# A second chunk by seven products in mixer B's output projection, and more weight sums by transfers

## The chip, the core and the metric

One core of a Trainium2 chip runs the whole kernel. The metric is the time of one launch on the device in microseconds; the median of three runs counts. The core's engines work from their own instruction streams and wait for one another by semaphores: TensorE (PE in the profile; PEld is its load of the stationary operand) multiplies matrices into PSUM, VectorE (DVE) and ScalarE (ACT) do elementwise work, GpSimd (POOL) a little of it, and SyncE (SP) issues nearly all loads of weights. GpSimd's queue also issues transfers, among them those that add to their destination.

## The reference

It is an encoder of two layers over 256 positions of width 2048, in float32. Each layer adds a token mixer and a gated MLP to the residual stream, each behind an RMS norm:

```python
h = x
for i in range(DEPTH):
    hn = rms_norm(h, mix_norm[i])
    ...
    h = h + (mixer_a or mixer_b)(hn, ...)   # A in layer 0, B in layer 1
    h = h + conv_ffn(rms_norm(h, ffn_norm[i]), w_up[i], conv_w[i], conv_b[i], w_down[i])
return rms_norm(h, final_norm)
```

Mixer B computes `qkv = h @ w_qkv` (2048 by 9216), dilated sliding-window attention in three groups of eight heads with a relative bias, weighs the groups, and projects `y @ w_o` (3072 by 2048). The MLP is `u = h @ w_up` (2048 by 11264), a depthwise convolution of width three over positions, `silu(gate) * val`, and `@ w_down` (5632 by 2048).

## The kernel before

**Precision.** A float32 product is made of three TensorE products. A weight block `raw` (128 partitions by 1024) is split into a high part `wh`, a rounded copy by ScalarE (line 128), and a low part `wl = raw - wh` by VectorE (line 129), and the activations are split the same way; PE then multiplies high by high, low by high and high by low. Every weight of the model goes through this once, and it is most of what ScalarE and VectorE do. `raw` blocks live in six buffers that are reused in the order in which they came free. Split pieces live in a ring of NHL = 3 pairs, and four in the down-projections, which add one.

**Seven products.** A projection works on column blocks of 512 outputs and on "chunks" of 512 inputs. The two halves of the positions (128 rows each) and a pair of column blocks form a 2 by 2 block product, and for some chunks it is done by seven products with sums of the blocks instead of eight (`project_pair`, line 215). A unit of work is either a column unit `("c", chunk, i)`, four 128x512 positions of the plain product (12 matmuls), or a product unit `("P", chunk, p)` with p from 1 to 7 (6 matmuls). The list `units` is the order of PE's work. The weight operands of products 1, 2, 3 are the chunk's blocks 11, 21, 22; those of 5, 7, 6, 4 are sums that are made in place: 11 += 12, 12 += 22, 22 += 11, 21 += 22 (`sums_behind`, lines 255 to 268). Each sum is an addition of 128x1024 by VectorE (line 253), or a transfer on GpSimd's queue that adds to its destination (`onto`, line 249): from DRAM into 12 (the sum for product 7), or from block 22 into 21 in SBUF (for product 4). The argument `by_dma` names the products whose sums go by transfer; without it VectorE makes all four, one unit ahead (`prepare`, line 270).

**Who uses it.** In each FFN the down-projection runs in two halves, six and five chunks long, and each half over two pairs of column blocks. The first pair of a half starts while the last activations are still being made ("late"). Chunks 0, 2 and 4 of the first half and 0 and 2 of the second go by seven products. The function `weave` spreads the column units of the other chunks among the products: evenly in the first half, after every product in the second. The first halves make one sum per chunk by transfer (7), the second halves two (7 and 4). Ahead of a second half's up-projection stands a block of seven of its own (`seven`, line 405, with the units of lines 735 to 739). Mixer B's output projection (`out_proj`, line 870) has six chunks and two pairs; chunk 2 goes by products, with all four sums on VectorE. Its activation sums are made by `make_forms` (line 427) behind the last heads.

**What sets the order.** The units and the order of the code fix PE's and GpSimd's streams. Small jobs (residual sums, convolution, forms) are generators that `step()` advances between units. A scheduler then orders each engine's instructions, and the splits and sums of weights are put 45 places ahead (`high_priority`). SP issues the loads in order: a load whose buffer isn't free yet holds up those behind it. At the end of a pair `combine` (line 555) adds the product accumulators to the residual stream; accumulators not made of products are added at line 576. `place_blocks` (line 386) copies transposed blocks; a string of four letters says which engine takes each copy ("p" GpSimd, "a" ScalarE, "v" VectorE).

## Time and profile before

| | |
|---|---|
| median of 3 runs | 2234.03 us (2233.73 to 2235.28) |
| the profiled execution | 2236.12 us, span 2234.3 us, granted clock 0.998 |
| first FFN, first half's down-projection, pair 1 and pair 2 | about 527 to 589 and 589 to 652 us |
| first FFN, block of seven ahead of the second half | about 652 to 696 us |
| mixer B's output projection, pair 1 and pair 2 | about 1387 to 1454 and 1454 to 1518 us |
| second FFN, first half's down-projection, pair 1 and pair 2 | about 1780 to 1842 and 1842 to 1904 us |

A row of a timeline begins with its start and duration in microseconds; a bracket at its end is the time that the engine idled before it, and what ended the wait. A group's row ends with busy time, mean nanoseconds of one, and idle time before it. A row of the windows has each engine's busy time in the stretch with its instructions in brackets, then the granted clock, the share of the transfer engines and GB/s.

### The profile page before, as it was taken

To read this page: it belongs to the slowest core of one execution; us is meant where nothing else is said; L and a number is where in the kernel's file an instruction comes from. 1 tells how busy PE (TensorE), PEld (TensorE's weight loads), DVE (VectorE), ACT (ScalarE), POOL (GpSimd) and SP (SyncE) were. 2 spreads that over 40 slices of the span, in tenths; PEclk is the share of its full clock that TensorE was granted. 3 is DMA by queue.
4 is the path that set the end of the run, shared out by engine and by line. 5 is a ranking of instruction groups with operands and counts; after the bars stand their busy time and mean duration, and the time that the engine had idled before them with its cause. 6 is when DMAs were issued, how large, how long until landed. Compare 5 with 4: busy or idle time off the path is not lost. (4 is left out here: it accounts for less than half of the span.)

```text
span 2234.3 us, 29271 instructions
## 1 busy us (share of the span) xinstructions
PE 2218.5 (99%) x9997; PEld 1835.6 (82%) x9997; DVE 1848.7 (83%) x2543; ACT 1563.9 (70%) x2411; POOL 349.9 (16%) x507
## 2 busy tenths in 40 slices
PE   9999999999999999999999999999999999999998
PEld 7888888888778888888888888888888888888886
DVE  6777778889998888879877988796888899988897
ACT  6665677777557777767876877576777765677764
POOL 2211112211001111111340213010101100001111
PEclk9999999999999999999999999999999999999999
DMA  8444656766766556766655565555665677665675
GB/s 301 160 151 148 202 189 211 233 209 190 234 213 209 194 195 192 244 204 204 217 179 191 170 207 173 189 194 187 195 195 192 205 224 221 208 195 191 222 235 163
DMA packets 129670, 448.99 MB, mean 201 GB/s; under 512 B 17664, under 2 KB 18432, under 8 KB 129520
## 3 DMA queue, kind: packets, MB, share of 16 engines
q1 hardware_dynamic: 119744, 425.64, 57.9%
q0 software_dynamic: 9344, 20.92, 4.9%
q8 instruction: 78, 1.28, 0.2%
q14 instruction: 72, 0.59, 0.1%
q10 hardware_dynamic: 432, 0.56, 0.1%
HBM read 438.11 MB, written 6.29 MB: 199 GB/s over the span
## 5 line engine op out<-in xcount | busy, mean ns | idle before, releaser
L129 DVE TENSOR_TENSOR wl<-raw,wh 128x1024 fp32r<-128x1024 f32 x873 | 1068.6, 1233 | 265.5 <-ACT wh L128 261.5
L128 ACT ACTIVATE wh<-raw 128x1024 fp32r<-128x1024 f32 x873 | 915.6, 1057 | 457.3 <-PE acc L155 162.9
L154 PE MATMUL acc<-wl,xh 128*128 128x512 f32 x1664 | 649.3, 390 | 2.4 <-DVE wl L165 2.1
L153 PE MATMUL acc<-wh,xh 128*128 128x512 f32 x1664 | 649.0, 391 | 0.0
L155 PE MATMUL acc<-wh,xh 128*128 128x512 f32 x1664 | 648.8, 390 | 0.0
L154 PEld LDWEIGHTS acc<-wl,xh 128*128 128x128 f32 x1664 | 313.0, 188 | 68.6 <-DVE wl L165 2.6
L155 PEld LDWEIGHTS acc<-wh,xh 128*128 128x128 f32 x1664 | 312.7, 188 | 64.4
L153 PEld LDWEIGHTS acc<-wh,xh 128*128 128x128 f32 x1664 | 312.8, 188 | 64.0
L318 PE MATMUL acc<-wh,ah 128*128 128x512 f32 x730 | 284.7, 390 | 0.6 <-DVE h L576 0.6
L320 PE MATMUL acc<-wh,al 128*128 128x512 f32 x730 | 284.3, 389 | 0.0
L393 POOL COPY u<-t 32x256 f32<-32x256 f32 x176 | 110.5, 628 | 804.2 <-DVE t L628 796.1
L323 PE MATMUL acc<-wl,ah 128*128 128x512 f32 x730 | 205.2, 390 | 0.5 <-DVE wl L129 0.5
L318 PE MATMUL acc<-wh,xh 128*128 128x512 f32 x416 | 162.8, 391 | 0.0
L320 PE MATMUL acc<-wh,xh 128*128 128x512 f32 x416 | 162.0, 389 | 0.0
L318 PEld LDWEIGHTS acc<-wh,ah 128*128 128x128 f32 x730 | 137.0, 188 | 30.1 <-DVE h L576 1.4
L323 PEld LDWEIGHTS acc<-wl,ah 128*128 128x128 f32 x730 | 136.7, 188 | 30.2 <-DVE wl L129 2.0
L395 ACT ACTIVATE u<-t 32x256 f32<-32x256 f32 x352 | 147.7, 420 | 18.3 <-DVE t L628 10.5
L320 PEld LDWEIGHTS acc<-wh,al 128*128 128x128 f32 x730 | 137.1, 188 | 28.3
L323 PE MATMUL acc<-wl,xh 128*128 128x512 f32 x416 | 113.1, 390 | 0.0
L318 PEld LDWEIGHTS acc<-wh,xh 128*128 128x128 f32 x416 | 78.1, 188 | 16.5 <-DVE h L576 0.4
L323 PEld LDWEIGHTS acc<-wl,xh 128*128 128x128 f32 x416 | 78.0, 188 | 16.2
L320 PEld LDWEIGHTS acc<-wh,xh 128*128 128x128 f32 x416 | 78.1, 188 | 16.0
(270 smaller groups left out, 2486.5 us busy)
## 6 DMA issues: line engine op xcount, KB each, us to landing
raw<-in_w_up_dram SPq DMA_DIRECT2D x352, 512.0 KB, 4.4
raw<-in_w_down_dram SPq DMA_DIRECT2D x176, 512.0 KB, 5.0
raw<-in_w_b_dram SPq DMA_DIRECT2D x144, 512.0 KB, 4.6
raw<-in_w_bo_dram SPq DMA_DIRECT2D x48, 512.0 KB, 4.5
raw<-in_w_a_dram SPq DMA_DIRECT2D x40, 512.0 KB, 4.5
raw<-in_w_ao_dram SPq DMA_DIRECT2D x32, 512.0 KB, 3.8
raw<-in_w_down_dram POOLq DMA_DIRECT2D x17, 512.0 KB, 6.3
raw<-in_w_a_dram SPq DMA_DIRECT2D x16, 256.0 KB, 5.4
```

The source lines that it names most:

```text
L128: nc.scalar.activation(wh, r, AF.Copy)
L129: nc.vector.tensor_tensor(wl, r, wh.bitcast(F32), ALU.subtract)
L153: nc.tensor.matmul(accs[m], xh, wh[:, j, :], start=st, stop=False)
L154: nc.tensor.matmul(accs[m], xh, wl[:, j, :], start=False, stop=False)
L155: nc.tensor.matmul(accs[m], xl, wh[:, j, :], start=False, stop=sp)
L318: nc.tensor.matmul(acc[k], xh, wh[:, j, :], start=k in fresh, stop=False)
L320: nc.tensor.matmul(acc[k], xl, wh[:, j, :], start=False, stop=False)
L323: nc.tensor.matmul(acc[k], xh, wl[:, j, :], start=False, stop=last[k] == i and j == 1)
L393: nc.gpsimd.tensor_copy(dst, src)
L395: nc.scalar.activation(dst, src, AF.Copy)
```

## The change

1. The output projection of mixer B does two chunks, 2 and 1, by seven products instead of chunk 2 alone, and both take two of their four weight sums by transfer (7 and 4). The products come in the order `ORDER_D`; in the first pair a column unit stands behind products 2, 3, 5 and 6, in the second behind every product while there are any. The forms of chunk 2 are started before the last head group's values, those of chunk 1 behind them, in tiles of their own.
2. In both FFNs' first-half down-projections, chunks 0 and 2 take two sums by transfer instead of one; chunk 4 stays at one.
3. In these halves `weave` puts a column unit behind products 3 and 6 only (first pair), or 3, 5 and 6 (second pair), instead of spreading them evenly. What is left stands at the end of the pair.
4. The block of seven ahead of a second half starts with two column units instead of one.
5. For the last pair of gate and value blocks in each half, the copies that VectorE made in `place_blocks` go to ScalarE ("paaa" for "pava"): eight copies in each of four halves.
6. A constant tile `ones` is filled by GpSimd at the start and not read.

```diff
--- before.py
+++ after.py
@@ -25,6 +25,7 @@
 ORDER_D = (1, 2, 3, 5, 6, 7, 4)
+BY_DMA = ({0: (7, 4), 2: (7, 4), 4: (7,)}, {0: (7, 4), 2: (7, 4)})
 PLACE = "pava"
@@ -213,7 +216,7 @@
     def project_pair(w, n0, n1, lhs, forms, units, late, early_done, n0_done, product_done=None, tail=False,
-                     lazy=False, by_dma=()):
+                     lazy=False, by_dma=None):
         home = {1: "M1", 2: "C11", 3: "C12", 4: "C21", 5: "M5", 6: "M6", 7: "M7"}
@@ -255,15 +258,15 @@
                 add(kg, "11", "12")
-                if 7 in by_dma:
+                if 7 in by_dma[kg]:
                     onto(kg, "12", w[n1, kg][:, 1024:])
...
                 add(kg, "22", "11")
-                if 4 in by_dma:
+                if 4 in by_dma[kg]:
                     onto(kg, "21", "22")
-            elif p == 6 and 4 not in by_dma:
+            elif p == 6 and 4 not in by_dma[kg]:
                 add(kg, "21", "22")
@@ -292,7 +295,7 @@
                     sums_behind(*units[i - 1][1:])
-                free = (5, 7, 4) + (6,) * (4 in by_dma)
+                free = (5, 7, 4) + (6,) * (4 in by_dma.get(kg, ()))
             else:
@@ -627,7 +630,7 @@
                 yield
-                place_blocks(u.rearrange("p j (m t) -> p j m t", m=2), t, PLACE)
+                place_blocks(u.rearrange("p j (m t) -> p j m t", m=2), t, "paaa" if n % NPAIR in (HALVES[0][1] - 1, HALVES[1][1] - 1) else PLACE)
                 yield
@@ -733,10 +736,10 @@
                         c = [("c", k, 2 * n + i) for n in range(2) for k in kgs[1:] for i in range(2)]
-                        units = c[:1]
+                        units = c[:2]
                         for i, f in enumerate(ORDER):
-                            units += [("P", 0, f)] + c[1 + i:2 + i] * (i < 5)
-                        units += c[6:]
+                            units += [("P", 0, f)] + c[2 + i:3 + i] * (i < 5)
+                        units += c[7:]
                         cs = []
@@ -820,13 +823,15 @@
                         c = c0[:-1] + c1[:4] + c0[-1:] + c1[4:-2]
-                    units = []
-                    units += [c.pop(0) for _ in range(lead)]
+                    units = [c.pop(0) for _ in range(lead)]
                     rest = len(c)
                     for i, u in enumerate(ps):
-                        n = min(1, len(c))
-                        if hf == 0 or late:
+                        if hf == 0:
+                            n = u[2] in ((3, 6) if late else (3, 5, 6))
+                        elif late:
                             n = (i + 1) * rest // len(ps) - i * rest // len(ps)
+                        else:
+                            n = min(1, len(c))
                         units += [u] + [c.pop(0) for _ in range(n)]
@@ -846,7 +851,7 @@
                                        lambda a: start(combine(a, n0, n1, fp, "s", combined)),
-                                       lambda a: first_half(a, n0, n1), tail=tail, by_dma=(7, 4) if hf else (7,))
+                                       lambda a: first_half(a, n0, n1), tail=tail, by_dma=BY_DMA[hf])
                     accs = acc["C12"], acc["C22"]
@@ -886,29 +891,30 @@
 
-            acc = project_pair(w, n0, n1, slots, lambda kg: forms, units, late_at,
-                               lambda a: start(combine(a, n0, n1, pool, "stg", combined, 2)), n0_done, lazy=True)
+            acc = project_pair(w, n0, n1, slots, forms.get, units, late_at,
+                               lambda a: start(combine(a, n0, n1, pool, "stg", combined, 2)), n0_done, lazy=True,
+                               by_dma=dict.fromkeys(forms, (7, 4)))
             done((acc["C12"], acc["C22"]), n1)
...
         if forms is not None:
-            sk = kgs[1]
-            kgs = [k for k in kgs if k != sk]
-            early = len(kgs) - late
+            kgs = [k for k in kgs if k not in forms]
+            early = 2
 
...
 
-            def woven(c, lead):
-                units = c[:lead]
-                for i, p in enumerate(ORDER):
-                    units += [("P", sk, p)] + c[lead + i:lead + i + 1]
-                return units + c[lead + 7:]
+            def woven(c, lead, behind):
+                units = [c.pop(0) for _ in range(lead)]
+                for k in forms:
+                    for p in ORDER_D:
+                        units += [("P", k, p)] + [c.pop(0) for _ in range(p in behind)]
+                return units + c
 
...
             head = columns(kgs[:early], 0) + columns(kgs[:early], 1)
-            pair(0, 1, head + woven(c0[:5] + c1[:3] + c0[5:] + c1[3:], 0), len(head))
+            pair(0, 1, head + woven(c0[:2] + c1[:2] + c0[2:] + c1[2:], 0, (2, 3, 5, 6)), len(head))
             c0, c1 = (columns(kgs, n) for n in range(2))
-            pair(2, 3, woven(c0[:8] + c1[:2] + c0[8:] + c1[2:], 1), None)
+            pair(2, 3, woven(c0 + c1, 1, ORDER_D), None)
             return hTn, ss
@@ -1164,6 +1170,15 @@
             kgs = list(range(4))
+            forms = {2: {}, 1: {}}
+
+            def form_tiles(*tags):
+                xs, ts = (bp.tile([P, 4, NT], F32, tag="stg", name=nm("xs"), bufs=2) for _ in range(2))
+                if len(tags) == 1:
+                    t = bp.tile([P, 4, 2, NT], F32R, tag=tags[0], name=nm("fm"))
+                    return xs, ts, [(t[:, i, 0], t[:, i, 1]) for i in range(4)]
+                t = [bp.tile([P, 4, NT], F32R, tag=g, name=nm("fm")) for g in tags]
+                return xs, ts, [(t[i // 2][:, i % 2 * 2], t[i // 2][:, i % 2 * 2 + 1]) for i in range(4)]
 
@@ -1323,16 +1338,12 @@
                 for g in range(3):
-                    start(v_gen(g, project(w_b, 6 * g + 4 + hf, hT, kgs)))
-            forms = {}
-
-            def form_tiles():
-                xs, ts = (bp.tile([P, 4, NT], F32, tag="stg", name=nm("xs"), bufs=2) for _ in range(2))
-                fm = bp.tile([P, 4, 2, NT], F32R, tag="bt0", name="fm")
-                return xs, ts, [(fm[:, i, 0], fm[:, i, 1]) for i in range(4)]
-
-            start(make_forms(forms, slots, 8, form_tiles))
-            return out_proj(w_bo, slots, [0, 2, 4, 1, 3, 5], 3, 3, junk, bp, ("vl", "kTh"), forms)
+                    va = project(w_b, 6 * g + 4 + hf, hT, kgs)
+                    if hf == 1 and g == 2:
+                        start(make_forms(forms[2], slots, 8, lambda: form_tiles("bt0")))
+                    start(v_gen(g, va))
+            start(make_forms(forms[1], slots, 4, lambda: form_tiles("qTl", "qTh")))
+            return out_proj(w_bo, slots, [0, 4, 1, 2, 3, 5], 3, 3, junk, bp, ("vl", "kTh"), forms)
```

**ScalarE in the first pair of the first FFN's first half, from product 2 of chunk 2 to product 2 of chunk 4.** A `wh` row is one unit's piece. Before, `raw_1041` is block 22 of chunk 2 (products 3 and 6) and `raw_1062` is block 21 of chunk 4 (product 2):

```order
L128 ACTIVATE wh_1039_5298<-raw_1038_5296 128x1024
L128 ACTIVATE wh_1042_5310<-raw_1041_5308 128x1024
L128 ACTIVATE wh_1044_5321<-raw_1031_5262 128x1024
L128 ACTIVATE wh_1047_5333<-raw_1046_5331 128x1024
L128 ACTIVATE wh_1049_5349<-raw_1041_5308 128x1024
L128 ACTIVATE wh_1051_5360<-raw_1032_5264 128x1024
L128 ACTIVATE wh_1053_5370<-raw_1038_5296 128x1024
L128 ACTIVATE wh_1056_5382<-raw_1055_5380 128x1024
L338 ACTIVATE fm_1097_5574<-u_539_2616 128x256
L128 ACTIVATE wh_1060_5402<-raw_1058_5398 128x1024
L338 ACTIVATE fm_1098_5575<-u_539_2616 128x256
L128 ACTIVATE wh_1063_5416<-raw_1062_5412 128x1024
```

Now `raw_1038` is block 22 of chunk 2 and `raw_1059` is block 21 of chunk 4:

```order
L131 ACTIVATE wh_1036_5282<-raw_1035_5278 128x1024
L131 ACTIVATE wh_1039_5294<-raw_1038_5292 128x1024
L131 ACTIVATE wh_1042_5308<-raw_1041_5304 128x1024
L131 ACTIVATE wh_1044_5324<-raw_1031_5264 128x1024
L131 ACTIVATE wh_1049_5346<-raw_1048_5344 128x1024
L131 ACTIVATE wh_1046_5334<-raw_1038_5292 128x1024
L131 ACTIVATE wh_1051_5362<-raw_1032_5266 128x1024
L131 ACTIVATE wh_1053_5372<-raw_1035_5278 128x1024
L341 ACTIVATE fm_1097_5576<-u_539_2618 128x256
L131 ACTIVATE wh_1057_5386<-raw_1055_5382 128x1024
L341 ACTIVATE fm_1098_5577<-u_539_2618 128x256
L131 ACTIVATE wh_1060_5400<-raw_1059_5396 128x1024
```

Both lists have two column units. They stood behind product 5 of chunk 2 (`raw_1046`) and right ahead of chunk 4 (`raw_1055`); now they stand behind product 3 (`raw_1041`) and ahead of product 6 (`raw_1048`), and chunk 4's first two products follow chunk 2's last one directly.

**SP at the same place, with what each load waits for.** `DMASW` is a transfer on GpSimd's queue, `DMAHW` one on SP's, the rest are engines. Before:

```order
L136 DMA raw_1055_5380<-in_w_down_dram 128x1024 [waits DMAHW3_49,DVE_49,Activation_49]
L136 DMA raw_1058_5398<-in_w_down_dram 128x1024 [waits DMAHW1_49,DVE_49,Activation_49]
L136 DMA raw_1059_5400<-in_w_down_dram 128x1024 [waits DMAHW6_49,DVE_49]
L136 DMA raw_1062_5412<-in_w_down_dram 128x1024 [waits DMAHW5_49,DMAHW2_49,DVE_49]
L136 DMA raw_1065_5426<-in_w_down_dram 128x1024 [waits DMASW0_49,DVE_49]
L136 DMA raw_1068_5444<-in_w_down_dram 128x1024 [waits DMAHW4_49,DVE_49]
```

Now:

```order
L139 DMA raw_1055_5382<-in_w_down_dram 128x1024 [waits DMAHW5_49,DVE_49]
L139 DMA raw_1056_5384<-in_w_down_dram 128x1024 [waits DMAHW1_49,DVE_49]
L139 DMA raw_1062_5410<-in_w_down_dram 128x1024 [waits DMAHW6_49,DVE_49]
L139 DMA raw_1059_5396<-in_w_down_dram 128x1024 [waits DMAHW2_49,DMAHW4_49,DMASW2_49,DVE_49]
L139 DMA raw_1065_5422<-in_w_down_dram 128x1024 [waits DMAHW3_49,DMASW1_49,DVE_49]
L139 DMA raw_1072_5461<-in_w_down_dram 128x1024 [waits DVE_49]
```

The load of `raw_1059` now waits for a transfer of GpSimd's queue (`DMASW2`), the one that adds `raw_1038` to `raw_1035`, since it takes over the buffer of `raw_1038`; two loads that stood with no such wait are now behind it.

**ScalarE where the second pair of that half ends and the block of seven begins.** Before, `raw_1162` is the last product's block and `raw_1214` that of the block's first product:

```order
L128 ACTIVATE wh_1181_5996<-raw_1180_5994 128x1024
L128 ACTIVATE wh_1183_6012<-raw_1162_5900 128x1024
L128 ACTIVATE wh_1187_6031<-raw_1186_6029 128x1024
L128 ACTIVATE wh_1212_6078<-raw_1211_6076 128x1024
L128 ACTIVATE wh_1215_6096<-raw_1214_6094 128x1024
L128 ACTIVATE wh_1219_6110<-raw_1218_6108 128x1024
```

Now they are `raw_1159` and `raw_1217`:

```order
L131 ACTIVATE wh_1180_5996<-raw_1159_5884 128x1024
L131 ACTIVATE wh_1184_6015<-raw_1183_6013 128x1024
L131 ACTIVATE wh_1187_6035<-raw_1186_6033 128x1024
L131 ACTIVATE wh_1212_6080<-raw_1211_6078 128x1024
L131 ACTIVATE wh_1215_6098<-raw_1214_6096 128x1024
L131 ACTIVATE wh_1218_6116<-raw_1217_6114 128x1024
```

Between the two there stood two column units (one of the pair, one of the block); now there are four.

More of the change, by code (lines that the diff above doesn't have):

```diff
@@ L52, in tile_encoder @@
     nc.gpsimd.memset(nhalf, -0.5)
+    ones = cpool.tile([P, P], F32, name="ones")
+    nc.gpsimd.memset(ones, 1.0)
     nc.scalar.dma_start(gain, gains)
```

## The prediction

> **What bounds the kernel now.** I read the page's busy times first, then what TensorE waited for, then the stages, then single waits.
>
> ```profile
> PE 2218.5 (99%) x9997; PEld 1835.6 (82%) x9997; DVE 1848.7 (83%) x2543; ACT 1563.9 (70%) x2411; POOL 349.9 (16%) x507
> PE ps L318 <- DVE cu L569: 1.5, 1, 1.5
> PE acc L318 <- DVE h L576: 0.6, 2, 0.4
> PE acc L323 <- DVE wl L129: 0.5, 2, 0.3
> ```
>
> TensorE (PE) is busy 99% of the span. The lower rows are its own waits (total, times, longest): in the stages that the change touches they come to 2.6 us in five places. So there are two ways to gain: give PE fewer matmuls, or remove those few waits. There are many ways to lose, since whatever makes a weight piece late is a new wait. The price of one matmul is the distance between two starts, not the 0.39 us that a row shows, since they overlap:
>
> ```profile
> 1401.64 0.39 PE L318 MATMUL acc<-wh,ah 128*128 128x512 f32 x1
> 1401.87 0.39 PE L320 MATMUL acc<-wh,al 128*128 128x512 f32 x1
> ```
>
> That is 0.227 us (1401.64 to 1401.87, and the rows before and after keep this step). A column unit (12 matmuls) is 2.72 us of PE, a product unit (6) is 1.36 us. Now the stages, by windows: stretch, its length, then the busy time of PE, PEld, DVE, ACT, POOL. The two first-half pairs of the first FFN come first, then its block of seven, the second half's first pair, and the two pairs of mixer B's output projection.
>
> ```profile
> 527.00:589.00 62.00, 62.00 (x275) 51.06 (x274) 60.33 (x72) 42.98 (x56) 5.40 (x8) 1.00 0.73 215
> 589.00:652.00 63.00, 62.33 (x273) 50.63 (x272) 58.14 (x60) 34.59 (x35) 2.68 (x4) 1.00 0.78 235
> 871.00:977.00 106.00, 106.00 (x470) 87.76 (x469) 88.68 (x114) 72.97 (x112) 13.41 (x20) 1.00 0.72 222
> 1387.00:1454.00 67.00, 67.00 (x306) 55.20 (x305) 49.31 (x55) 36.97 (x49) 2.39 (x4) 1.00 0.57 190
> 1454.00:1518.00 64.00, 64.00 (x284) 52.95 (x284) 54.32 (x69) 42.98 (x65) 6.59 (x8) 1.00 0.61 198
> 1780.00:1842.00 62.00, 61.91 (x273) 50.87 (x271) 60.86 (x73) 42.92 (x56) 5.37 (x8) 1.00 0.74 220
> 560.00:580.00 20.00, 20.00 (x90) 16.53 (x89) 19.93 (x22) 14.08 (x18) 0.97 (x2) 1.00 0.86 255
> 1455.00:1475.00 20.00, 20.00 (x90) 16.57 (x89) 19.52 (x26) 16.94 (x30) 4.20 (x4) 1.00 0.42 132
> ```
>
> In the first-half pairs VectorE (DVE) is busy 60.33 of 62 us: there the two engines run level, and weights come just in time. The out-projection has slack on the whole (49.31 of 67, 54.32 of 64), with one tight piece (19.52 of 20).
>
> **Fewer matmuls: -2.72 us.** A chunk costs a pair of column blocks four column units (48 matmuls), or seven products (42). One more chunk by products, in both pairs of the out-projection, is 12 matmuls fewer, and nothing else changes PE's count. 12 x 0.227 = 2.72 us, if PE stays the bound in that stage; 0 if it does not (below). The granted clock is 1.00 in all these rows, so the step holds.
>
> **The wait ahead of the block of seven: -1.64 us.** These are PE's rows around it:
>
> ```profile
> 655.70 0.39 PE L320 MATMUL acc<-wh,xh 128*128 128x512 f32 x1
> 657.57 0.50 PE L318 MATMUL ps<-wh,xh 128*128 128x512 f32 x1 [1.48 <-DVE cu L569]
> ```
>
> The start is 1.87 us behind the one before, 1.64 more than a step. The first product needs a PSUM bank that VectorE still reads for the last pair's sums. Between the pair's last product and this one PE has two column units now (one of the pair, one ahead of the block), 5.4 us; the changed order has four, 10.9 us, for the pair ends on two columns and the block begins with two. 5.4 us more than a wait of 1.6: it goes whole unless VectorE falls 3.8 us further behind, and its load falls. Bounds -1.64 and 0; I take -1.64. The second FFN shows no such wait, so nothing is gained there.
>
> **The waits in the four first-half pairs: -1.74 us.** These are all of them, the first FFN's and the second's:
>
> ```profile
> 590.21 0.50 PE L318 MATMUL acc<-wh,ah 128*128 128x512 f32 x1 [0.39 <-DVE h L576]
> 606.42 0.73 PE L323 MATMUL acc<-wl,ah 128*128 128x512 f32 x2 [0.27 <-DVE wl L129]
> 1842.08 0.50 PE L318 MATMUL acc<-wh,ah 128*128 128x512 f32 x1 [0.17 <-DVE h L576]
> 1858.30 0.74 PE L323 MATMUL acc<-wl,ah 128*128 128x512 f32 x2 [0.27 <-DVE wl L129]
> ```
>
> A bracket counts from the row's modelled end, 0.16 us later than the next step would be, so four brackets (1.10) stand for 1.74 us. All four end at VectorE, so what matters is its load. Groups of instructions (busy, mean ns, idle before):
>
> ```profile
> L129 DVE TENSOR_TENSOR wl<-raw,wh 128x1024 fp32r<-128x1024 f32 x873 | 1068.6, 1233 | 265.5 <-ACT wh L128 261.5 <-PE ps L519 0.5 <-issue 0.2
> L397 DVE COPY u<-t 32x256 f32<-32x256 f32 x176 | 64.9, 369 | 5.9
> L253 DVE TENSOR_TENSOR raw<-raw,raw 128x1024 f32<-128x1024 f32 x46 | 57.1, 1241 | 0.5
> L395 ACT ACTIVATE u<-t 32x256 f32<-32x256 f32 x352 | 147.7, 420 | 18.3 <-DVE t L628 10.5
> L339 DVE TENSOR_TENSOR al<-cv,ah 128x256 fp32r<-128x256 f32 x82 | 32.4, 419 | 0.5 <-ACT ah L338 0.5
> L128 ACT ACTIVATE wh<-raw 128x1024 fp32r<-128x1024 f32 x873 | 915.6, 1057 | 457.3 <-PE acc L155 162.9 <-PE acc L320 132.7 <-DMA raw<-in_w_down_dram 43.5
> ```
>
> Each pair loses two sums at 1.241 (2.5 us), and the first pair of each half also eight copies at 0.369 (3.0 us; they become 3.4 us of ScalarE, which is busy 42.98 of 62). So 60.33 becomes 54.8 of 62, 58.14 becomes 55.7 of 63. VectorE no longer sets the pace; I take -1.74. If the copies, now ahead of the first pieces on ScalarE, hold these up instead, it is 0.
>
> **A new chain in the same pairs: +3.0 us.** Here is what the second sum costs by transfer. The second half's pair already does it (VectorE's split of product 3 and the sum behind it, GpSimd's issue, the next load on the in-order SP queue; then the median time of loads to landing, the spread over all 22 transfers that GpSimd's line issues, and ScalarE's waits in this stage):
>
> ```profile
> 883.91 1.22 DVE L129 TENSOR_TENSOR wl<-raw,wh 128x1024 fp32r<-128x1024 f32 x1
> ...
> 885.38 1.22 DVE L253 TENSOR_TENSOR raw<-raw,raw 128x1024 f32<-128x1024 f32 x1
> 887.17 0.86 POOL L249 DMA_DIRECT2D raw<-raw  x1 [7.57 <-DVE raw L253]
> 893.77 0.33 SPq L136 DMA_DIRECT2D raw<-in_w_down_dram  x1
> raw<-in_w_down_dram SPq DMA_DIRECT2D x176, 512.0 KB, 5.0
> DMA to landing us min/median/max: 4.5/6.4/7.6
> ACT wh L128 <- DMA raw<-raw: 3.5, 2, 2.2
> ```
>
> The transfer reads block 22 of its chunk, whose buffer one of the next chunk's loads reuses; that load waits on SP until it has landed. In the changed first-half pair this is the load for product 2 of the next chunk. From the split of product 3: 1.47 us to the sum's start (883.91 to 885.38), 1.79 to the issue (887.17), 6.4 to landing, 5.0 for the load, 1.06 for its ScalarE copy: 15.7 us. PE needs the piece six products and two columns later: 60 matmuls, 13.6 us, plus whatever lead the pieces had at product 3. So the price of a place is 2.1 us less the lead. In the pair shown above, 72 matmuls (16.3 us) lie between and no wait of PE stands there (all of them are quoted here), which agrees. There are two places in each FFN where only two columns are woven in (chunk 0 to 2, 2 to 4 of the first pair): four in all. The second pairs weave three columns in (16.3 us) and are safe. The lead: in 560 to 580 us VectorE is busy 19.93 of 20, so today there is none; yet ScalarE's copies over the whole run wait mostly for PE to give a buffer back (162.9 and 132.7 us), less for data (43.5), so where VectorE has time the few split pieces in flight (four here) are all ready. I take a lead of one product, 1.36: 0.75 x 4 = 3.0. Bounds 0 (lead over 2.1) and 4 x 3.3 = 13.2 (no lead, landing at 7.6).
>
> By the Trainium skill, "DMA: Bandwidth & Descriptors", Anatomy of one DMA, a transfer on GpSimd's path takes about 2.0 us plus its bytes at 436 GB/s, an estimate of 3.2 us for 512 KB. With that the chain would be 12.2 us and cost nothing. The trace has a median of 6.4 and nothing under 4.5, and it decides.
>
> **In the out-projection: +0.8, and ahead of it +0.3.** Six more splits on VectorE (6 x 1.233 = 7.4 us) and 12 more form operations, most of them ahead of the stage (12 x 0.42 = 5.0), against 128 us with 103.6 busy: covered on average, and its sums by VectorE stay at eight. But only three pieces are in flight here, and the evacuations of the last heads stand among the first products' pieces on ScalarE and VectorE. Bounds 0 and +2.72 (the saving eaten); I take 0.8, nearer to 0 since no wait is seen in either window now. The second forms' 5.0 us on a VectorE that runs 19.52 of 20 in places: bounds 0 and 1, I take 0.3.
>
> **Sum.** -2.72 - 1.64 - 1.74 + 3.0 + 0.8 + 0.3 = -2.0 us. The profiled run took 2236.12 (span 2234.3), so 2234.1; the median shown is 2234.03, so 2232.0.
>
> **Rivals.**
> A, the chain is hidden: a lead of 2.1 us or more at all four places, since VectorE is freed by 5.5 us in the pair. For it: split pieces usually wait for PE. Against it: the first pieces come late behind the moved copies. Then -6.1 plus half of the last two terms, 0.55: -5.5, 2228.5.
> B, the chain decides (the other side): no lead at the four places, and landings at 7.6, because the DMA share there is 0.86 already and more transfers come. 13.2 in place of 3.0: +8.2, 2242.2. From 2.4 us a place on, the kernel is slower by over 0.2%. For it: the load that waits holds up every load behind it on SP. Against it: the second half's pair lives with the same chain at 0.72.
> C, the saved matmuls only turn into waits, VectorE being the bound of the out-projection: 2.72 instead of 0.8, 2233.9. Against it: 103.6 of 131.
>
> **How the numbers follow.** Forecast 44%, A 31%, B 14%, C 11%. 0.2% is 4.5 us (2229.6 to 2238.5), about what a measurement of this kernel can tell from no change. Nearly all of A and a little of the forecast is faster, 0.32; nearly all of B and little else slower, 0.14; the rest same, 0.54. The likeliest case alone spans 2229.6 to 2236; the range takes in A with all its terms (2228.0, and 1 us for the runs' own spread) and B's milder part: 2227 to 2238.5.
>
> **What would show it.** Right: PE's count falls by 12, the row of PE's wait for cu L569 (now three lines lower) is gone, PE waits for wh or ScalarE's wh waits for in_w_down behind a raw<-raw landing between the third product of chunk 2 and the second of chunk 4 in both FFNs, near 570 and 1820 us. Wrong: no PE wait there (A), or waits of 2 us and more in all four (B). A stall over 1 us among the first products of the out-projection would make its term too small.

## The result and the profile after

The changed kernel takes 2268.5 us (median of 4 runs, 2264.2 to 2270.18), the kernel before 2234.66 us (4 runs, 2233.73 to 2235.44): a ratio of 1.0149, interval 1.0131 to 1.0166. It is slower by 33.8 us. The prediction was 2232.0 with a range up to 2238.5, so it is wrong in sign and far outside its range. Later runs of the kernel before, beside the experiments, have medians of 2234.5 to 2235.7. One execution of a later experiment (the two sums with four columns) took 4791.66 us in a slow state and is not in its median.

First the busy times after (engine, busy us, share of the span, instructions) and TensorE's waits for more than 2 us in all:

```profile
span 2267.8 us, 29350 instructions
...
PE 2231.8 (98%) x9985; PEld 1834.3 (81%) x9985; DVE 1836.1 (81%) x2521; ACT 1579.9 (70%) x2453; POOL 361.1 (16%) x524
...
PE acc L321 <- ACT wh L131: 11.4, 10, 2.1
PE acc L157 <- DVE wl L132: 3.9, 8, 1.0
PE acc L326 <- DVE wl L132: 3.1, 6, 1.2
PE acc L157 <- DVE wl L168: 2.4, 1, 2.4
PE ps L356 <- DVE al L342: 2.2, 1, 2.2
```

The matmul count is down by 12 (9997 to 9985), as it should be, yet PE's busy time is up by 13 us (in part because some of its matmuls run slower, see the end). VectorE's is down by 12.6 us. So the work moved as the diff says, and PE waits for weights: it had no wait of this kind for ScalarE before, and now has ten. What ScalarE itself waits for shows why (the kernel before had 43.5 and 8.0 us in these two rows):

```profile
ACT wh L131 <- DMA raw<-in_w_down_dram: 67.7, 43, 6.3
ACT wh L131 <- DMA raw<-raw: 30.9, 9, 5.3
```

To see where the time went, I took from each trace the first matmul of every stage and its lag behind the same matmul of the kernel before. The table has the growth of that lag in each stretch, in us, one profile each; it is what experiments below are read by. A profile's first matmul differs by up to 3 us from run to run, and this is left out.

| stretch | changed | only copies | only two sums | projection alone | places and lead |
|---|---|---|---|---|---|
| up to FFN 1's first pair | +0.9 | +1.2 | -0.1 | +0.4 | +0.4 |
| FFN 1, first pair | +5.3 | +4.1 | +5.6 | -0.1 | +1.0 |
| FFN 1, second pair | +4.1 | +1.3 | +2.5 | -0.7 | -0.4 |
| FFN 1, block of seven to second half's first pair | -0.9 | +1.7 | +1.1 | -1.2 | -1.5 |
| second half's pairs | +1.3 | +1.9 | 0.0 | 0.0 | 0.0 |
| mixer B up to the projection | +3.8 | +0.2 | +0.2 | +3.6 | 0.0 |
| projection, first pair | +3.0 | 0.0 | 0.0 | +1.2 | 0.0 |
| projection, second pair | +5.8 | 0.0 | 0.0 | +3.5 | 0.0 |
| FFN 2 up to its first pair | +0.9 | +0.9 | 0.0 | 0.0 | 0.0 |
| FFN 2, first pair | +5.2 | +5.6 | +6.3 | +0.6 | +1.1 |
| FFN 2, second pair | +2.1 | +1.6 | +1.0 | +0.2 | +1.0 |
| FFN 2, block of seven and after | +0.6 | +1.0 | +1.3 | +0.4 | +0.6 |

In the changed kernel half of the loss (16.7 us) is in the four first-half pairs, and 12.6 us are at the projection. Here is the worst place of FFN 1's first pair, where product 4 of chunk 2 begins: ScalarE's copies, GpSimd's transfers, and PE.

```profile
562.07 1.06 ACT L131 ACTIVATE wh<-raw 128x1024 fp32r<-128x1024 f32 x1 [0.65 <-DVE raw L256]
564.67 1.06 ACT L131 ACTIVATE wh<-raw 128x1024 fp32r<-128x1024 f32 x1 [1.54 <-PE acc L326]
570.99 1.06 ACT L131 ACTIVATE wh<-raw 128x1024 fp32r<-128x1024 f32 x1 [5.26 <-DMA raw<-raw]
```

```profile
562.58 0.86 POOL L252 DMA_DIRECT2D raw<-raw  x1 [2.54 <-DVE raw L256]
```

```profile
569.71 0.61 PE L326 MATMUL acc<-wl,ah 128*128 128x512 f32 x2
572.10 0.50 PE L321 MATMUL acc<-wh,ah 128*128 128x512 f32 x1 [1.78 <-ACT wh L131]
```

The transfer leaves at 562.58 and ScalarE has its result at 570.99: 8.4 us. What waits for it is the piece of product 4 of the same chunk, whose block the transfer itself makes, and here not the next chunk's load that the prediction priced. That load is a link of the same chain, though, one chunk earlier. The transfer of chunk 0 lands at 551.24; SP issues the load for chunk 2's product 2 directly behind that, and ScalarE waits for it and for the one behind it:

```profile
551.31 0.33 SPq L139 DMA_DIRECT2D raw<-in_w_down_dram  x1
```

```profile
555.17 1.06 ACT L131 ACTIVATE wh<-raw 128x1024 fp32r<-128x1024 f32 x1 [1.21 <-DMA raw<-in_w_down_dram]
557.17 1.06 ACT L131 ACTIVATE wh<-raw 128x1024 fp32r<-128x1024 f32 x1 [0.93 <-DMA raw<-in_w_down_dram]
```

So chunk 2 comes to product 3 with no lead: PE starts it at 558.28, as its piece is ready, and the transfer for product 4 leaves 4.3 us behind that. In FFN 1's second pair the priced load reaches PE itself. The transfer of chunk 0 lands there at 614.72, and product 2 of chunk 2 is late:

```profile
614.78 0.33 SPq L139 DMA_DIRECT2D raw<-in_w_down_dram  x1
```

```profile
618.77 1.06 ACT L131 ACTIVATE wh<-raw 128x1024 fp32r<-128x1024 f32 x1 [1.94 <-DMA raw<-in_w_down_dram]
```

```profile
619.88 0.50 PE L321 MATMUL acc<-wh,ah 128*128 128x512 f32 x1 [0.58 <-ACT wh L131]
```

### The profile page after: what moved, and what is told of

Read it like the earlier page. It is cut to its first block, busy times and chain, and to the rows that moved or that the text cites. A ratio compares the mean times of both kernels' runs of the same rounds, so it can differ in the third digit from the quotient of the medians.

```text
span 2267.8 us, 29350 instructions
## 1 busy us (share of the span) xinstructions
PE 2231.8 (98%) x9985; PEld 1834.3 (81%) x9985; DVE 1836.1 (81%) x2521; ACT 1579.9 (70%) x2453; POOL 361.1 (16%) x524
## 5 line engine op out<-in xcount | busy, mean ns | idle before, releaser
L321 PE MATMUL acc<-wh,ah 128*128 128x512 f32 x710 | 280.6, 395 | 12.2 <-ACT wh L131 11.4
L323 PE MATMUL acc<-wh,al 128*128 128x512 f32 x710 | 279.1, 393 | 0.0
L398 ACT ACTIVATE u<-t 32x256 f32<-32x256 f32 x384 | 161.1, 420 | 17.9 <-DVE t L631 9.4
L321 PEld LDWEIGHTS acc<-wh,ah 128*128 128x128 f32 x710 | 134.4, 189 | 46.6 <-ACT wh L131 17.9
L326 PEld LDWEIGHTS acc<-wl,xh 128*128 128x128 f32 x416 | 77.9, 188 | 16.4 <-DVE wl L132 0.3
```

Source lines behind the costliest of these rows:

```text
L321: nc.tensor.matmul(acc[k], xh, wh[:, j, :], start=k in fresh, stop=False)
L323: nc.tensor.matmul(acc[k], xl, wh[:, j, :], start=False, stop=False)
L326: nc.tensor.matmul(acc[k], xh, wl[:, j, :], start=False, stop=last[k] == i and j == 1)
L398: nc.scalar.activation(dst, src, AF.Copy)
```

## The experiments

Each edit is against the changed kernel or the kernel before, as its text says. "Copies" are the 32 block copies of part 5, "sums" the second sums of part 2, "places" the column units of part 3, "lead" part 4.

### Parts taken away from the changed kernel

**The first halves as before.**

```diff
-BY_DMA = ({0: (7, 4), 2: (7, 4), 4: (7,)}, {0: (7, 4), 2: (7, 4)})
+BY_DMA = ({0: (7,), 2: (7,), 4: (7,)}, {0: (7, 4), 2: (7, 4)})
...
-                        if hf == 0:
-                            n = u[2] in ((3, 6) if late else (3, 5, 6))
-                        elif late:
+                        if hf == 0 or late:
```

> The first halves' down-projections as before in both FFNs (one sum per chunk by transfer, column units spread evenly); the output projection, the lead of two columns and the moved copies stay as changed. Theory (the chain of transfers costs the time there): the four pairs give back what they lost between the two traces, 5.3 + 4.1 + 5.2 + 2.1 = 16.7 us, so about 2252 us. Rival (the copies moved to ScalarE hold up the first pieces of these pairs): they still lose most of it, 2262 us or more.

Measured: 2260.3 us (ratio to before 1.0109, 1.0094 to 1.0124). Only 8 us came back, and the two first pairs still lose 4.4 and 5.3 us. So something else loses there, and only the copies are left: the rival, though it said 2262 us or more, is right for these two.

**One sum by transfer, new places kept** (only the first of the two edits above).

> As changed, but the first halves' second sum per chunk (21 += 22) is made by VectorE again; the new places of the column units stay. Theory (the second transfer is the cause): the waits for raw<-raw there are gone and most of 16.7 us comes back, 2252 to 2255 us; the loads issued beside the former transfers land in about 5 us instead of 7 to 9. Rival (products now stand close together, and pieces come too slowly for them whoever adds): 2262 us or more.

Measured: 2253.63 us (1.0080, 1.0064 to 1.0097): 14.9 us come back, as the theory said. It is 6.7 us faster than with the places undone too, so the new places help.

**Even places, two sums kept** (only the second edit).

> As changed, but the first halves' column units are spread evenly again; the second sum stays a transfer. Theory (the transfer's length decides, and with even spreading as many columns stand between a chunk's product 3 and product 4): 10 us or more of the loss stay, 2262 to 2270 us. Rival (the new places of the column units are the cause): 2252 to 2255 us.

Measured: 2273.83 us (1.0172, 1.0157 to 1.0187), slower than the changed kernel by 5. The places are no cause of the loss; they soften it.

**The projection as before.** All of its part is put back; the core of it:

```diff
-            kgs = [k for k in kgs if k not in forms]
+            sk = kgs[1]
+            kgs = [k for k in kgs if k != sk]
...
-            return out_proj(w_bo, slots, [0, 4, 1, 2, 3, 5], 3, 3, junk, bp, ("vl", "kTh"), forms)
+            return out_proj(w_bo, slots, [0, 2, 4, 1, 3, 5], 3, 3, junk, bp, ("vl", "kTh"), forms)
```

> As changed, but mixer B's output projection and its forms as before: one chunk by products, all sums by VectorE. Between the two traces 3.6 us were lost ahead of it, 3.0 in its first pair and 6.7 from its second pair to the second FFN's down-projection. Theory (all of this is the output projection's): 13.3 us come back, about 2255 us. Rival (a part of it is a late start carried over from the first FFN, or the changed copies of the second FFN): less than 9 us come back, 2260 us or more.

Measured: 2256.08 us (1.0089, 1.0074 to 1.0104): 12.4 us come back, near the theory's 13.3.

**The copies on VectorE again.**

```diff
-place_blocks(..., t, "paaa" if n % NPAIR in (HALVES[0][1] - 1, HALVES[1][1] - 1) else PLACE)
+place_blocks(..., t, PLACE)
```

> As changed, but the 32 copies go to VectorE again (pava for paaa). In the runs so far each stretch ahead of a first pair lost 0.9 to 1.3 us and the first pairs 4.4 and 5.3 us with one sum and the old spreading, where nothing but the copies had changed. Theory (moved copies hold up the first pieces on ScalarE, and VectorE idles behind them): 5 us or more come back, 2256 to 2263 us. Rival (VectorE needs the room that they gave, as the prediction had it): nothing comes back, 2267 us or more.

Measured: 2252.11 us (1.0075, 1.0060 to 1.0090): 16.4 us come back, more than either side expected. By the medians this is the largest single part, and the prediction had it as a gain.

**The forms behind the last heads.**

```diff
                     va = project(w_b, 6 * g + 4 + hf, hT, kgs)
-                    if hf == 1 and g == 2:
-                        start(make_forms(forms[2], slots, 8, lambda: form_tiles("bt0")))
                     start(v_gen(g, va))
+            start(make_forms(forms[2], slots, 8, lambda: form_tiles("bt0")))
             start(make_forms(forms[1], slots, 4, lambda: form_tiles("qTl", "qTh")))
```

> As changed, but the forms of chunk 2 are started behind the last head group's values (as before), not ahead of them. Theory (the forms' work stands ahead of the last heads' on VectorE, and TensorE waits 2.2 us for it with 3.6 us lost in all ahead of the projection): 3 us come back, about 2265 us. Rival (the forms are then late for the first product, and the wait moves there): no change, 2267 to 2270 us.

Measured: 2261.43 us (1.0114, 1.0097 to 1.0131): 7 us come back, but not where I said. Ahead of the projection 2.8 of the 3.6 us are still lost; the first pair loses 0.1 instead of 3.0.

**Block 22's buffer given back later.**

```diff
-                free = (5, 7, 4) + (6,) * (4 in by_dma.get(kg, ()))
+                free = (5, 7, 4)
...
             if kind == "P" and p in free:
                 blocks.pop((kg, b))
+            if by_dma and kind == "P" and p == 4 and (kg, "22") in blocks:
+                done_raw(blocks.pop((kg, "22")))
```

> As changed, but block 22's buffer is given back behind product 4 instead of product 6, so the next chunk's load for product 2 takes another buffer and no longer waits for the transfer; a later load does. Theory (the load behind the transfer, the chain that the prediction priced): most of the 14.9 us that the second sums cost come back, 2254 to 2260 us. Rival (product 4's own piece, which the transfer makes, is what comes late, and neighbouring loads are slowed by it): 2265 us or more.

Measured: 2277.52 us (1.0189, 1.0174 to 1.0204), 9 us slower than the changed kernel. TensorE's and ScalarE's waits in this kernel:

```profile
PE acc L323 <- ACT wh L131: 18.3, 11, 4.6
...
ACT wh L131 <- DMA raw<-raw: 36.8, 10, 5.6
```

The waits for the transfer grew (30.9 to 36.8 us), but this does not clear the load that the prediction named. It had another buffer now, yet it still stood behind the transfer: SP's order had changed too, and the load that takes over block 22's buffer was issued directly ahead of it. These are SP's waits for the transfers from 520 to 660 us, in the changed kernel and in this one:

```profile
SPq L139 <- DMA raw<-raw: 19.7, 4, 6.2
```

```profile
SPq L139 <- DMA raw<-raw: 18.3, 4, 6.5
```

In FFN 1's first pair, for example, the transfer lands at 548.58, SP's next load (into block 22's buffer) goes out at 548.65, and the one for product 2 at 549.07. So this run doesn't decide between theory and rival. That the 9 us come from holding one of only six buffers longer is likely, and not shown.

**One sum by transfer in the projection.** `by_dma=dict.fromkeys(forms, (7,))` for `(7, 4)`.

> As changed, but the output projection makes the sum 21 += 22 on VectorE and only the sum for product 7 by transfer. Theory (the chain of the second sum costs there too): 4 us or more of what the two pairs lose come back, 2260 to 2264 us. Rival (the ring of three and the forms are what costs): 2266 us or more.

Measured: 2261.91 us (1.0125, 1.0110 to 1.0140): 6.6 us come back. The second pair then loses 1.1 us instead of 5.8, the first gains 0.1. The second sum costs here too; the 3.6 us that stay ahead of the projection are put down to the forms by the rows there, since no run takes the forms away alone.

### Parts alone, on the kernel before

**The places and the lead.**

```diff
-                        units = c[:1]
+                        units = c[:2]
...
-                        if hf == 0 or late:
+                        if hf == 0:
+                            n = u[2] in ((3, 6) if late else (3, 5, 6))
+                        elif late:
```

> As before but for the new places of the column units in the first halves and the lead of two columns ahead of the blocks of seven: one sum by transfer, copies on VectorE, output projection as before. Theory (these two parts are the good ones): the wait ahead of the block of seven, 1.64 us, and some of the 1.74 us in the four pairs go, 2231 to 2233 us against 2235. Rival (products close together need VectorE's room, which is busy 60.33 of 62 us there): 2237 us or more.

Measured: 2236.89 us over 10 runs (1.0009, 1.0000 to 1.0019). The block of seven gains 1.5 us, the pairs lose 2.6. That is just under the rival's bound and nearer to it than to the theory, at the edge of what these runs can tell from no change. The wait in both first pairs is for VectorE's `wl` (0.47 and 0.46 us), which fits the rival: the products stand closer than VectorE can follow when nothing has been taken off it.

**The copies alone.** The line with `"paaa"` of the change, and no other.

> As before, but the 32 copies on ScalarE (paaa for pava), and nothing else of the change. Theory (by themselves they cost what undoing them gave back, because VectorE idles 3.6 us behind ScalarE's copies at the start of a pair in which it has no room): 2245 to 2250 us. Rival (they hurt only together with the second sums): 2238 us or less.

Measured: 2253.01 us (1.0082, 1.0067 to 1.0097), 18.5 us slower. VectorE's rows at the start of FFN 1's first pair, then ScalarE's, in this kernel, and last VectorE's before:

```profile
528.80 1.42 DVE L132 TENSOR_TENSOR wl<-raw,wh 128x1024 fp32r<-128x1024 f32 x1
532.10 1.23 DVE L132 TENSOR_TENSOR wl<-raw,wh 128x1024 fp32r<-128x1024 f32 x1 [1.89 <-ACT wh L131]
...
536.27 1.23 DVE L132 TENSOR_TENSOR wl<-raw,wh 128x1024 fp32r<-128x1024 f32 x1 [1.68 <-ACT wh L131]
```

```profile
528.79 2.20 ACT L398 ACTIVATE u<-t 32x256 f32<-32x256 f32 x5
531.01 1.06 ACT L131 ACTIVATE wh<-raw 128x1024 fp32r<-128x1024 f32 x1
532.09 3.06 ACT L398 ACTIVATE u<-t 32x256 f32<-32x256 f32 x7
535.18 1.06 ACT L131 ACTIVATE wh<-raw 128x1024 fp32r<-128x1024 f32 x1
```

```profile
529.43 0.28 DVE L397 COPY u<-t 32x256 f32<-32x256 f32 x1
529.75 1.30 DVE L129 TENSOR_TENSOR wl<-raw,wh 128x1024 fp32r<-128x1024 f32 x1
531.09 1.29 DVE L397 COPY u<-t 32x256 f32<-32x256 f32 x3
```

Before, VectorE and ScalarE shared the copies and neither waited long. Now ScalarE makes twelve in two bunches with one split piece between them, and VectorE idles 1.89 + 1.68 = 3.6 us behind these pieces, to save 3.0 us of its own. In a stretch where it was busy 60.33 of 62 us it falls behind: the sum-making transfer for product 7 of chunk 2 leaves 30.5 us behind the pair's first matmul (557.40) instead of 28.2 (555.97 before). Most of the pair's loss then stands at one place, product 6 of chunk 2. ScalarE's and PE's rows there, then ScalarE's row for that piece before:

```profile
564.77 2.00 ACT L131 ACTIVATE wh<-raw 128x1024 fp32r<-128x1024 f32 x2 [5.35 <-DMA raw<-in_w_down_dram]
```

```profile
566.83 0.50 PE L321 MATMUL acc<-wh,ah 128*128 128x512 f32 x1 [1.90 <-ACT wh L131]
```

```profile
561.19 1.06 ACT L128 ACTIVATE wh<-raw 128x1024 fp32r<-128x1024 f32 x1 [3.10 <-DVE raw L253]
```

Before, ScalarE copied product 6's piece as soon as VectorE had summed it, and then waited for the transfer for product 7's. With the copies moved, the scheduler's order has these two the other way round: ScalarE stands 5.35 us for the transfer (it lands at 564.67), and product 6's piece, whose sum VectorE starts at 560.16, comes second. The second FFN's first pair has the same pause (2.70 us), with doubled matmul steps behind it (see the end). The first FFN's second half loses 1.9 us in its own pairs too.

**The copies to GpSimd** (`"papa"` for `"pava"` at the same places).

> As before, but the 32 copies that the change moved go to GpSimd (625 ns each by the trace before) instead of ScalarE. Theory (ScalarE's copies hold up the first weight pieces; freeing VectorE is no harm in itself): 2232 to 2238 us, some 15 us less than with ScalarE. Rival (the copies are late wherever they are moved, and the last activations and forms with them): 2245 us or more.

Measured: 2238.07 us over 10 runs (1.0017, 1.0007 to 1.0026). 15 us less than with ScalarE, as the theory said, but still 3.5 us slower than before: relieving VectorE of the copies brings nothing. VectorE idles some 3.2 us in the stretch shown above here too, and PE has no pause at product 6. So idle time of VectorE alone isn't the price; pieces that come late are, and the order of ScalarE's copies.

**The two sums alone, even places.** The line is shown against the same program with one sum per chunk, which works as the kernel before:

```diff
-BY_DMA = ({0: (7,), 2: (7,), 4: (7,)}, {0: (7, 4), 2: (7, 4)})
+BY_DMA = ({0: (7, 4), 2: (7, 4), 4: (7,)}, {0: (7, 4), 2: (7, 4)})
```

> As before, but two sums by transfer for chunks 0 and 2 of the first halves, columns spread evenly, copies on VectorE. Theory (a transfer that sums in SBUF comes too late for product 4 even where the pair is otherwise undisturbed): 7 us or more are lost, 2242 us or more; PE waits for wh behind raw<-raw. Rival (only the delay by the copies leaves no lead; alone the sums free 2.5 us of VectorE per pair): 2233 to 2237 us.

Measured: 2252.61 us (1.0083, 1.0067 to 1.0098), 18.1 us slower. ScalarE's waits of this kernel:

```profile
ACT wh L131 <- DMA raw<-raw: 42.7, 10, 6.7
ACT wh L131 <- DMA raw<-in_w_down_dram: 34.8, 30, 4.3
```

It isn't only the copies' delay that makes the sums late: alone, with even places, they wait longer than in the whole change (42.7 against 30.9 us). PE's longest pauses are at product 4 of chunk 2 in both first pairs, 3.8 and 3.2 us, with doubled steps behind them.

**The two sums with four columns between products 3 and 4.** Shown against the changed kernel's line:

```diff
-                            n = u[2] in ((3, 6) if late else (3, 5, 6))
+                            n = u[1] != 4 and u[2] in (3, 5, 6, 7)
```

> As before, with two sums by transfer for chunks 0 and 2 of the first halves (which alone cost 18 us), but a column unit behind each of products 3, 5, 6 and 7 of these chunks, so that four columns stand between product 3 and product 4, 16.3 us of TensorE's work instead of 8 to 11. Copies on VectorE, the rest as before. Theory (the transfer is late for its own product 4, and distance cures it): the waits behind raw<-raw go, 2234 to 2240 us, the upper end since chunk 4's products then stand without columns. Rival (the transfers slow the loads beside them, or VectorE, whatever the distance): 2246 us or more.

Measured: 2251.68 us over 3 runs (1.0077, 1.0060 to 1.0094). The waits changed, and the time did not:

```profile
ACT wh L131 <- DMA raw<-in_w_down_dram: 83.8, 39, 6.3
...
ACT wh L131 <- DMA raw<-raw: 7.1, 3, 3.2
```

Distance does cure the transfer's own lateness (42.7 to 7.1 us), but the loads come late instead (34.8 to 83.8). Issues with their median time to landing tell why; first a stretch of this kernel with one summing transfer, then the same stretch (541 to 546 us) of the kernel before, then the same kind of place (605 to 608 us) in the changed kernel:

```profile
raw<-in_w_down_dram SPq DMA_DIRECT2D x3, 512.0 KB, 6.9
raw<-raw POOLq DMA_DIRECT2D x1, 512.0 KB, 7.7
```

```profile
raw<-in_w_down_dram SPq DMA_DIRECT2D x2, 512.0 KB, 4.8
```

```profile
raw<-in_w_down_dram SPq DMA_DIRECT2D x3, 512.0 KB, 8.8
raw<-raw POOLq DMA_DIRECT2D x1, 512.0 KB, 9.7
```

At these places a load that is issued beside the transfer lands about when it does, 2 to 4 us slower than in the stretch of the kernel before. Over the whole changed kernel the difference is smaller: loads of `w_down` issued within 3 us behind such a transfer land in a median of 6.4 us (30 loads, up to 9.0), those beside no summing transfer in 4.9 (138 loads). Both theories are thus half right. A part of what is still lost is the edit's own: chunk 4's seven products now follow one another without columns, and the pauses at 588 to 597 us and at 1847 to 1854 us stand there. How much of the 17 us is the slowed loads and how much the crowding isn't settled.

**The projection's change alone** (as changed; the rest as before).

> As before, with the output projection's change alone (two chunks by products, two sums by transfer, early forms). Theory (what undoing it gave back from the full change is its own): 12 us lost, 2245 to 2249 us. Rival (part of that was the state in which the rest of the change left the kernel): 2241 us or less.

Measured: 2244.76 us (1.0050, 1.0033 to 1.0066), 10.1 us slower.

**The projection with less.** One sum by transfer, chunk 2's forms behind the last heads, chunk 1's started behind the drain ahead of the first products.

```diff
+                if drained:
+                    drained()          # starts make_forms(forms[1], ...)
```

> As before but for mixer B's output projection, which does chunks 2 and 1 by products with one sum per chunk by transfer; chunk 2's forms are started behind the last heads, chunk 1's only when the projection's first products begin. Theory (the loss ahead of and in the projection is the early forms and the second sum; without them the 12 matmuls show): 2231 to 2234 us. Rival (three pieces in flight are too few for products of two chunks): 2237 us or more.

Measured: 2239.41 us over 10 runs (1.0023, 1.0014 to 1.0033). Better than the projection's change as it was by 5 us, but still slower than before. The edit did not do all it says: the scheduler placed chunk 1's forms on VectorE ahead of the projection anyway, and TensorE's wait there remained:

```profile
PE ps L358 <- DVE al L344: 2.6, 1, 2.6
```

### The account

| | alone, on the kernel before | taken away from the changed kernel |
|---|---|---|
| copies to ScalarE | +18.5 | -16.4 |
| second sums | +18.1 (even places) | -14.9 |
| projection | +10.1 | -12.4 |
| places and lead | +2.0 | (places only) +5.3 |

The parts alone add up to 48.7 us, the change to 33.8. With the new places the sums cost about 5 us (copies undone: 2252.1 against 2234.9 is 17.2, less 10.1 and 2.0 for the other two parts) and the copies about 6 (sums undone: 2253.6 against 2235.7 is 17.9, less the same), but both together 21.7 (33.8 less 12.1). So each seems to take the little lead that the other needs. These sums are rough, though: each median carries some 3 us of uncertainty, and the copies alone stand with even places, where the order of products 6 and 7 on ScalarE costs them extra. No version tried is faster than the kernel before.

## Why the prediction was wrong, point by point

**The matmuls, -2.72 us: the count held, the saving did not show.** Twelve fewer are there, yet the projection's change costs 10.1 us by itself. Even without the second sum and with later forms it costs 4.9.

**The wait ahead of the block of seven, -1.64 us: right.** With places and lead alone this stretch is 1.5 us shorter, and no PE wait for cu stands there. In the whole change 0.9 is seen.

**The waits in the four pairs, -1.74 us, "0" at worst: the step that failed most.** I counted what VectorE gives up (3.0 us of copies) and set ScalarE's side against its idle share (42.98 of 62 busy). What matters is that VectorE's split of a piece waits for ScalarE's copy of it, and that the moved copies stand in line ahead of the first pieces. I even named that ("If the copies, now ahead of the first pieces on ScalarE, hold these up instead") and bounded it at 0, as if the most to lose was the gain. It cost 18.5 us alone (16.4 in the changed kernel). Alone, 4.1 and 5.6 us of it are in the first pairs, most of that in the pause at product 6 of chunk 2; the rest lies in the second pairs, the blocks of seven and the first FFN's second half (1.9 us).

**The chain, +3.0 us, bounds 0 to 13.2: the mechanism was there, but its nearer reader was left out.** The second sums cost 14.9 us in the changed kernel and 18.1 alone. I priced the next chunk's load that waits for the transfer. It does come late, as the rows at 551.31 and 614.78 show. Nearer by one unit stands product 4 of the same chunk, which reads the transfer's own result, and which I had at nothing: by the same rows 1.47 + 1.79 + 6.4 + 1.06 = 10.7 us from product 3's split, with 48 matmuls (10.9 us) in between in the changed first pairs. That is no margin at all, with a landing at its median of 6.4 us. The row of ScalarE's waits for raw<-raw that I quoted (3.5 us in two) was already this reader. The four landings in FFN 1's two pairs took 7.6, 8.3, 9.7 and 6.7 us, and the loads beside them were slowed too, which I had at 5.0. Where I called the second pairs safe (16.3 us) they lost 2.9 us in the first FFN and 0.8 in the second (4.1 and 2.1 against 1.2 and 1.4 with one sum). How the cost divides between the two readers and the slowed loads stays open, since the run with the later buffer did not take the load away from behind the transfer.

The pair in the second half that I took as proof has the same 48 matmuls between its products 3 and 4. It does not wait because it has a lead: ScalarE's copy for its first product 3 ends at 882.5 us and PE first uses it at 887.4. I read the missing wait there as proof of the distance. I also read 871 to 977 us as this pair alone; it holds both pairs of the half, and the first FFN's second one goes by plain products only. In the pair itself VectorE is busy 92% of the time, in the whole window 84%:

```profile
871.00:922.50 51.50, 51.50 (x229) 42.64 (x228) 47.24 (x57) 35.65 (x48) 6.04 (x8) 1.00 0.80 236
```

The rule of the Trainium skill that I weighed there ("DMA: Bandwidth & Descriptors", Anatomy of one DMA, an estimate of 3.2 us) was rightly set aside: the changed kernel's summing transfers in SBUF have a median of 6.7 us. (With 3.2 us the chain that I gave there comes to 12.5 us, not 12.2.) Of what the same page of the Trainium skill says under "Issuing engines are not separate DMA queues" (transfers from all engines run on the same 16 and interleave) the traces show the price here: a median of 6.4 us for loads beside such a transfer against 4.9, and 6.9 and 8.8 against 4.8 at the places shown. That sentence would have spoken against the change, and I did not use it.

**The projection, +0.8 and +0.3: far too small.** The forms ahead of it cost 3.6 us in the stretch. VectorE runs in order, and an evacuation (al) that PE's transposes wait for stands behind them: between 1396.04 and 1400.51 us VectorE runs six operations of the forms, 0.42 us each, and two splits without a pause, and then that al. I set the twelve added operations against VectorE's average room and not against what is queued behind them. The second sum then costs 6.6 us, and I had left the chain out here. Which wait it is isn't settled. PE's longest pause in the two pairs, 2.1 us at 1518.1, is behind this piece:

```profile
1517.00 1.06 ACT L131 ACTIVATE wh<-raw 128x1024 fp32r<-128x1024 f32 x1 [6.52 <-DMA raw<-in_w_bo_dram]
```

That is a load issued at 1509.29, beside the transfer for product 7 (1508.67 to 1516.71), and not a summing transfer in SBUF. With one sum the pause is gone.

**Rival B** (the chain decides, no lead) came nearest in direction, at 2242.2, and was given 14%. It had one of the three mechanisms. The chances followed from treating the other two as covered.

## What to carry to other kernels

Where two engines run level, ask of every moved instruction what is queued behind it on the engine that takes it, and who waits for that; an average share of busy time says nothing about the first pieces of a stage. A sum made by a transfer must be covered up to every reader of what it writes and every load that waits for what it reads, at the slow end of its landing times and not the median, and the loads issued beside it have to be priced as late too. A bound of 0 on a term needs a reason of its own: "it only loses the gain" was not one.

## What the runs showed of the hardware

**A pause of PE of some 2 us can be followed by about 3 us at half its clock.** This is the changed kernel behind the pause quoted above, then the granted clock (the figure behind POOL's busy time) before, in and behind that stretch:

```profile
574.38 0.63 PE L321 MATMUL acc<-wh,ah 128*128 128x512 f32 x1
574.80 0.63 PE L323 MATMUL acc<-wh,al 128*128 128x512 f32 x1
575.23 0.63 PE L321 MATMUL acc<-wh,ah 128*128 128x512 f32 x1
```

```profile
569.00:573.00 4.00, 2.22 (x10) 1.43 (x8) 0.92 (x1) 2.01 (x3) 0.00 (x0) 0.98 0.66 236
573.00:576.20 3.20, 3.20 (x9) 2.26 (x8) 3.20 (x6) 2.19 (x4) 0.00 (x0) 0.50 0.99 385
576.20:580.00 3.80, 3.72 (x17) 2.73 (x16) 3.80 (x5) 2.92 (x4) 0.85 (x1) 1.00 0.39 65
```

The step is 0.43 us instead of 0.23 and the clock reads 0.50. Over the traces of all 17 kernels, their starts left out, of 36 pauses of 1.93 us or more (beyond the usual step) 23 were followed by such a stretch (4 to 13 doubled steps), of 46 pauses between 1.0 and 1.93 us two. The price is 0.2 us a step, some 1.4 us for seven. The changed kernel has three of them (behind 570, 1398 and 1516 us), 23 doubled steps and so some 4.6 us of its 33.8; the kernel before has none after its start. So a stall that crosses some 2 us may cost more than its length, and whether it does changes from one place to the next. The Trainium skill ("TensorE: Matmul & The Clock Gate", What's actually happening) has the clock halve after an idle window of about 3.4 us, counted by a window that runs freely; the halving agrees with these rows, but here pauses well under 3.4 us were enough.
